# Mixer of a macaron block: rounding the queries and keys of six head pairs as whole tiles, and placing them by transfers

## The chip, the cores and the metric

The kernel runs on one core of one Trainium2 chip. The metric is device time in microseconds (us) for one execution. The kernel before was run three times: 890.2 us is the median, 889.88 and 890.86 the ends. The engines are named as in the profile: PE (TensorE, matrix multiplications), PEld (its weight loads), DVE (VectorE), ACT (ScalarE), POOL (GpSimd) and SP (SyncE, which here only issues transfers); "SPq" in a row is SP's queue of transfers.

## The reference, cut to what matters

```python
for layer in range(DEPTH):                       # DEPTH = 1, x is 512 x 1024, float32
    x = x + 0.5 * swiglu(rmsnorm(x, ffn1_norm), ffn1_w_gate, ffn1_w_up, ffn1_w_down)
    x = x + token_mixer(rmsnorm(x, mix_norm), w_in, w_out, ...)
    x = x + 0.5 * swiglu(rmsnorm(x, ffn2_norm), ffn2_w_gate, ffn2_w_up, ffn2_w_down)
return rmsnorm(x, final_norm)

def token_mixer(h, w_in, w_out, ...):            # 4 differential heads, 8 dilated heads
    qa, ka, va, qb, kb, vb = split(h @ w_in)     # head dimension 64
    oa = diff_attention(qa, ka, va, lam, bias)   # two maps per head: p0 - lam * p1, causal
    ob = dilated_attention(qb, kb, vb, bias)     # three dilations, joined into one softmax
    return concat(rmsnorm(oa) * (1 - lam0), ob) @ w_out
```

The scores are `q @ k.T * 64 ** -0.5` plus a bias, in float32. The change concerns only how q and k reach the score products.

## The kernel before, in words

The span has three stages: the first feed-forward block, the mixer (about 325 to 545 us into the span) and the second feed-forward block. Everything is held transposed: 128 partitions are 128 features, 512 columns are the tokens.

**Split products.** PE multiplies in the format fp32r, which is float32 rounded. Where one rounding is not enough, a value is split into a rounded high part (ACT copies it into an fp32r tile, which rounds it) and the rest (DVE subtracts), and a product is made of three products of parts (`mm3`, lines 152 to 154) or, for the scores, of two.

**The mixer.** A list `plan` names twelve steps, `v0 q0 q1 v1 q2 q3 q4 v2 q5 q6 v3 q7`, each of eight chunks of PE work (48 matmuls of 512 columns in a q step, 96 of 256 columns in a v step). A step `q u` projects the queries and keys of head pair `u` into two PSUM tiles, `pq` and `pk`; each holds two heads (or two maps of one differential head), one in partitions 0 to 63 (`lo`) and one in 64 to 127 (`hi`). There are eight pairs, 0 to 7; pairs 0 to 3 are differential heads. The rest of the mixer is fitted between these chunks by a table: `put(t, rank, f)` asks for step `f` at chunk `t`; steps of a rank under 10 are issued before the chunk, those of a rank of 10 or more behind it, in the order of their ranks. PE, DVE and ACT run their instructions in exactly that order. SP's order is chosen by a scheduler, and it too issues its transfers one after the other: a transfer whose wait isn't over holds up those behind it.

**What the scores read.** For pair `u` the scores need six tiles of 128 partitions: `q0` and `q1`, the two queries, each stacked as high part and rest (`q0`: high part in `lo`, rest in `hi`; `q1` the other way round); `k0` and `k1`, the high part of a key in both halves; `l0` and `l1`, the key's rest in both halves. `score(m, i)` (lines 1227 and 1228) makes, for map or head `m` and the block `i` of 128 queries, two matmuls: `k` against `q`, then `l` against `q`; `q` is the stationary operand. With `e` the last chunk of step `q u`, the first scores of pairs 1 to 6 come ahead of chunk `e + 6`; pairs 1 to 3 ask for both `m` at once, pair 6 for `m = 1` a chunk later, pairs 4 and 5 (named `STACKED`) four chunks later.

**How these tiles are filled before.** Behind chunk `e`, `scaled` (lines 1055 and 1057) takes `pq` and `pk` out of PSUM into `tq` and `tk`, two DVE instructions on 128 partitions. Then there are three ways:

- Pairs 0 and 7 (`evac_now`) do all halves by ACT and DVE. The change leaves them alone.
- Pairs 1 to 4: `evac_q` casts four halves of 64 partitions on ACT (lines 1063 to 1066) right behind chunk `e`; `evac_k` copies the other half of `k0` and `k1` by two transfers, makes the two rests of the keys on DVE (line 1078) and copies each by a transfer (line 1073); `evac_rests` makes the two rests of the queries on DVE (line 1085), a chunk later, writing them straight into `q0` and `q1`.
- Pairs 5 and 6 (`SPREAD`): the keys are cast as one tile `kh` of 128 partitions (line 1114), and their rest is made as one tile `kl` (line 1120); eight transfers of 64 partitions (line 1109) put them into `k0, k1, l0, l1`. The queries are done by halves in place (lines 1125 and 1129).

**What else is in the queues there.** ACT's exponentials of the scores (line 1232), its copies of transposed probabilities `ptb` (line 1256) for the products with the values (`po`, line 1267), its casts of weights (line 944) and of outputs `mh` (line 1307); DVE's score steps (line 1229), weight rests (line 948) and `tx` (line 1358); SP's weight loads (line 139) and bias strips (line 878).

Of the kernel before, what the change touches and what calls it, by code (L numbers as in the profile page):

```python
# [14 lines left out]
F32 = mybir.dt.float32  # L15
F32R = mybir.dt.float32r
# [12 lines left out]
NQ = S // P  # L29
# [53 lines left out]
def tile_macaron(ctx: ExitStack, tc, xs, xT, wf, wgu1, wst1, wd1, wdg1, wqk, wv, wo, wgu2, wst2, wd2,  # L83
# [13 lines left out]
    def slot(i, nm, dt=F32):  # L97
        return sl.tile([P, S], dt, tag=f"slot{i}", name=nm)
# [867 lines left out]
    vt = {}  # L966

    STACKED = (4, 5)
    SPREAD = (5, 6)
    SOONER = (2, 3)  # L970
    DIVS = ((1, 1, 1, 1), (1, 1, 1, 1))
    TURN_AT, VALUES_AT, NEXT = (5, 7, 8), (7, 10), 4
# [60 lines left out]
    def qk_chunks(u):  # L1033
# [12 lines left out]
        def tiles():  # L1046
            b0 = 31 + (u % 2) * 6
            qk[u] = [slot(b0 + i, f"{n}{u}", F32R)
                     for i, n in enumerate(("q0", "q1", "k0", "k1", "l0", "l1"))]
            return qk[u]  # L1050

        def scaled():
            tq = st["tq"] = slot(28, f"tq{u}")
            tk = st["tk"] = slot(30, f"tk{u}")
            V.scalar_tensor_tensor(flat(tq[:]), evens(st["pq"][:]), -(HD ** -0.5),
                                   flat(held["bc"][:]), op0=ALU.mult, op1=ALU.mult)
            V.tensor_tensor(flat(tk[:]), evens(st["pk"][:]), flat(held["bc"][:]), op=ALU.mult)
            return tq, tk

        def evac_q():  # L1060
            q0, q1, k0, k1, l0, l1 = tiles()
            tq, tk = scaled()
            A.copy(k0[lo, :], tk[lo, :])
            A.copy(k1[hi, :], tk[hi, :])
            A.copy(q0[lo, :], tq[lo, :])
            A.copy(q1[hi, :], tq[hi, :])

        def evac_k():
            q0, q1, k0, k1, l0, l1 = qk[u]
            tq, tk = st["tq"], st["tk"]  # L1070

            def other_half(t, a, b):
                nc.sync.dma_start(t[b, :].bitcast(F32), t[a, :].bitcast(F32))

            other_half(k0, lo, hi)
            other_half(k1, hi, lo)
            for a, b, kx, lx in ((lo, hi, k0, l0), (hi, lo, k1, l1)):
                V.tensor_tensor(lx[a, :], tk[a, :], kx[a, :].bitcast(F32), op=ALU.subtract)
                other_half(lx, a, b)

        def evac_rests():
            q0, q1, k0, k1, l0, l1 = qk[u]
            tq = st["tq"]
            for a, b, qx in ((lo, hi, q0), (hi, lo, q1)):
                V.tensor_tensor(qx[b, :], tq[a, :], qx[a, :].bitcast(F32), op=ALU.subtract)

        def evac_now():
            q0, q1, k0, k1, l0, l1 = tiles()
            tq, tk = scaled() if u != 7 else (st["tq"], st["tk"])
# [10 lines left out]
        if u == 7:  # L1100
            put(e, 11, scaled)
            put(e + 1, 2.5, evac_now)
        elif u in DIRECT:
            put(e, 11, evac_now)
        elif u in SPREAD:
            def send(t, *places):
                for o, a in zip(places, (lo, hi)):
                    for b in (lo, hi):
                        nc.sync.dma_start(o[b, :].bitcast(F32), t[a, :].bitcast(F32))

            def cast_k():
                q0, q1, k0, k1, l0, l1 = tiles()
                t = st["kh"] = slot(0, f"kh{u}", F32R)
                A.copy(t[:], st["tk"][:])
                send(t, k0, k1)

            def low_k():
                q0, q1, k0, k1, l0, l1 = qk[u]
                t = slot(1, f"kl{u}", F32R)
                V.tensor_tensor(t[:], st["tk"][:], st["kh"][:].bitcast(F32), op=ALU.subtract)  # L1120
                send(t, l0, l1)

            def cast_q(n):
                a = (lo, hi)[n]
                A.copy(qk[u][n][a, :], st["tq"][a, :])

            def low_q(n):
                a, b = ((lo, hi), (hi, lo))[n]
                V.tensor_tensor(qk[u][n][b, :], st["tq"][a, :], qk[u][n][a, :].bitcast(F32),
                                op=ALU.subtract)  # L1130

            put(e, 11, scaled)
            put(e + 1, 6.7, cast_k)
            put(e + 2, 7, low_k)
            for n in range(2):
                put(e + 2 + n, 6.7, cast_q, n)
                put(e + 3 + n, 11, low_q, n)
        else:
            put(e, 11, evac_q)
            put(e + 1, 11, evac_k)  # L1140
            put(e + 2, 7, evac_rests)
        return [lambda k=k: chunk(k) for k in range(KD)]

    mh, ml, whole, mixed = [None] * KD, [None] * KD, {}, [None] * 4
# [58 lines left out]
    def attention(u, s):  # L1203
# [205 lines left out]
        for i in range(NQ):  # L1409
            for m in range(2):  # L1410
                put(s + step * i + (0 if quick or diff else m), 6, score, m, i)
            put(s + step * i + (1 if quick else 3), 5, combine, i)
            if diff:
                put(tv + 2 * i, 2, turn, 0, i)
                put(tv + 2 * i + (3 if (u, i) in ((0, 0), (1, NQ - 1)) else 2), 1, values, 0, i)
            else:
                for m in range(2):
                    put(tv + step * i + (0 if quick else m), 2, turn, m, i)
                    put(tv + step * i + (1 if quick else m + 2), 1, values, m, i)
# [503 lines left out]
```

## Time and profile before

| what | value |
|---|---|
| median of three runs | 890.2 us |
| the profiled execution: its own time | 890.6 us |
| its span, first to last instruction | 887.7 us, so 2.9 us lie around it |
| mean granted TensorE clock | 0.997 |
| busy over the span: PE, DVE, ACT, POOL | 99%, 85%, 62%, 13% |
| mixer, 320 to 545 us: PE, DVE, ACT busy of 225 us | 222.77, 179.42, 146.44 us |
| DMA share in six stretches of 10 to 13 us in which q and k are placed | 0.44 to 0.76 |

A row of the timeline gives the start in us from the span's start, the time taken in us, the engine, the line, the operation, output<-inputs, shapes and the count; a bracket at the end gives the idle time before it and what ended it. PE's matmuls are pipelined: a matmul of 512 columns shows 0.38 us, but the next one starts 0.22 us after it, so that waits of PE are best read from one start to the next.

### The profile page before, as it was taken

Reading aid. Unit: us, or ns where it says so; the run is one execution under the profiler, and the core shown is the slowest. Engines: PE = TensorE matmul, PEld = TensorE weight load, DVE = VectorE, ACT = ScalarE, POOL = GpSimd, SP = SyncE. Lnnn points to the kernel's source line nnn. Section 1 sums busy time; section 2 is a strip of 40 time slices with the busy share of each in tenths; the row PEclk is TensorE's granted clock in tenths of the full one; section 3 lists DMA queues with packets and bytes.
Section 4 is the critical chain, followed back from the end, with each engine's and each line's share of the span. In section 5 each row is a group of like instructions: output and inputs, shape, how many; then the busy total and the mean of one; then the engine's idle time right before and its main releaser. Section 6 shows DMA issues by size and latency. Waiting matters only on the chain.

```text
span 887.7 us, 17743 instructions
## 1 busy us (share of the span) xinstructions
PE 875.6 (99%) x6558; PEld 834.5 (94%) x6558; DVE 755.1 (85%) x1590; ACT 550.7 (62%) x1162; POOL 111.2 (13%) x140
## 2 busy tenths in 40 slices
PE   9999999999999999999999999999999999999996
PEld 8889999999999999998989889889999999999996
DVE  7799998787998995788997859999899678799786
ACT  7456674455765764666766858466667355666474
POOL 0011101012103100001010220011110111211100
PEclk9999999999999999999999999999999999999998
DMA  8456756688857842445365664656783857884842
GB/s 279 125 168 157 177 142 184 148 212 213 201 141 211 222 132 95 119 131 156 106 174 149 183 139 120 176 158 152 185 212 97 201 169 187 216 224 118 215 127 95
DMA packets 65685, 146.85 MB, mean 165 GB/s; under 512 B 7632, under 2 KB 8912, under 8 KB 65600
## 3 DMA queue, kind: packets, MB, share of 16 engines
q1 hardware_dynamic: 47840, 113.02, 39.2%
q0 software_dynamic: 17616, 32.45, 22.7%
q8 instruction: 51, 0.84, 0.4%
q14 instruction: 34, 0.28, 0.1%
q10 hardware_dynamic: 144, 0.26, 0.1%
HBM read 137.28 MB, written 2.14 MB: 157 GB/s over the span
## 4 chain that ended last, share of the span: by engine, by line
PE 82%; DVE 10%; ACT 4%; issue 2%; DMA 1%; SPq 0%; DVEq 0%; ACTq 0%
PE po L1267 2%; PE pdb L154 1%; DVE w L948 1%; PE pdb L153 1%; PE pdb L152 1%; DVE w L445 1%; PE pv L1012 1%; PE pv L1014 1%; PE pv L1013 1%; PE pygb L152 1%; PE pwgb L154 1%; PE pxgb L154 1%; PE pyub L154 1%; PE pyub L153 1%; PE pxub L154 1%
## 5 line engine op out<-in xcount | busy, mean ns | idle before, releaser
L1232 ACT ACTIVATE pr<-pr,small 128x128 f32<-128x128 f32 (+3 forms) x64 | 35.7, 559 | 31.4 <-DVE small L1229 31.1
L441 ACT CAST w<-s2b 128x512 fp32r<-128x512 f32 x52 | 32.4, 623 | 22.0 <-DVE s2b L423 19.9
L441 ACT CAST w<-s2a 128x512 fp32r<-128x512 f32 x48 | 29.8, 623 | 23.3 <-DVE s2a L423 19.7
L445 DVE TENSOR_TENSOR w<-s2b,w 128x512 fp32r<-128x512 f32 x52 | 35.6, 685 | 0.9 <-ACT w L441 0.6
L1012 PE MATMUL pv<-w,xh 128*128 128x256 f32 x128 | 35.7, 279 | 0.0
L1229 DVE CUSTOM_DVE_ANT_0 pr<-sc,strip 128x128 f32<-128x128 f32 (+3 forms) x64 | 29.5, 485 | 7.2 <-PE sc L1228 7.0
L1014 PE MATMUL pv<-w,xh 128*128 128x256 f32 x128 | 35.1, 274 | 0.0
L1013 PE MATMUL pv<-w,xl 128*128 128x256 f32 x128 | 35.1, 274 | 0.0
L445 DVE TENSOR_TENSOR w<-s2a,w 128x512 fp32r<-128x512 f32 x48 | 32.8, 684 | 0.8 <-ACT w L441 0.6
L152 PE MATMUL pq<-xh,w 128*128 128x512 f32 x64 | 25.6, 401 | 0.0
L948 DVE TENSOR_TENSOR w<-raw_qk,w 128x512 fp32r<-128x512 f32 x32 | 21.7, 686 | 4.5 <-ACT w L944 4.5
L1013 PEld LDWEIGHTS pv<-w,xl 128*128 128x128 f32 x128 | 24.5, 191 | 0.1
L1012 PEld LDWEIGHTS pv<-w,xh 128*128 128x128 f32 x128 | 24.5, 191 | 0.1
L1014 PEld LDWEIGHTS pv<-w,xh 128*128 128x128 f32 x128 | 24.5, 191 | 0.0
L152 PE MATMUL pk<-xh,w 128*128 128x512 f32 x64 | 24.3, 380 | 0.0
L154 PE MATMUL pq<-xh,w 128*128 128x512 f32 x64 | 24.3, 379 | 0.0
L153 PE MATMUL pk<-xl,w 128*128 128x512 f32 x64 | 24.3, 379 | 0.0
L154 PE MATMUL pk<-xh,w 128*128 128x512 f32 x64 | 24.3, 379 | 0.0
L153 PE MATMUL pq<-xl,w 128*128 128x512 f32 x64 | 24.3, 379 | 0.0
L1267 PEld LDWEIGHTS po<-v,ptb 128*128 128x128 f32 x160 | 21.5, 191 | 2.6 <-ACT ptb L1256 1.6
L944 ACT CAST w<-raw_qk 128x512 fp32r<-128x512 f32 x32 | 19.3, 615 | 6.2 <-PE pv L1013 2.8
L1267 PE MATMUL po<-v,ptb 128*128 128x128 f32 (+1 forms) x160 | 22.0, 272 | 1.0 <-ACT ptb L1256 1.0
(826 smaller groups left out, 4096.5 us busy)
## 6 DMA issues: line engine op xcount, KB each, us to landing
raw_qk<-wqk_dram SPq DMA_DIRECT2D x16, 512.0 KB, 3.8
raw0bg<-wst_dram SPq DMA_DIRECT2D x9, 512.0 KB, 5.0
raw0bu<-wst_dram SPq DMA_DIRECT2D x9, 512.0 KB, 5.7
raw_gua<-wgu_dram SPq DMA_DIRECT2D x8, 512.0 KB, 3.6
raw0ag<-wst_dram SPq DMA_DIRECT2D x8, 512.0 KB, 5.0
raw0au<-wst_dram SPq DMA_DIRECT2D x8, 512.0 KB, 5.2
raw0ad<-wdg_dram SPq DMA_DIRECT2D x8, 512.0 KB, 5.9
strip<-bias_rows SPq DMA_DIRECT2D x16, 256.0 KB, 4.0
```

Source lines behind the costliest of these rows:

```text
L152: T.matmul(po, wh, mh, start=first, stop=False, skip_group_check=on)
L153: T.matmul(po, wh, ml, start=False, stop=False, skip_group_check=on)
L154: T.matmul(po, wl, mh, start=False, stop=last, skip_group_check=on)
L441: A.copy(made[t][0], source(t))
L445: V.tensor_tensor(l, source(t), h.bitcast(F32), op=ALU.subtract)
L948: V.tensor_tensor(l[:, c:c + 512], raw[:, c:c + 512], h[:, c:c + 512].bitcast(F32), op=ALU.subtract)
L1012: T.matmul(po, xh[k][:, xs], mh_, start=k == 0, stop=False)
L1013: T.matmul(po, xl[k][:, xs], mh_, start=False, stop=False)
L1014: T.matmul(po, xh[k][:, xs], ml_, start=False, stop=k == KD - 1)
L1229: V.tensor_tensor_reduce(out=o, in0=a, in1=b, op0=ALU.add, op1=ALU.min, scale=1.0, scalar=3.0e38, accum_out=st["mx"][:, m, i:i + 1])
L1232: A.activation(pi, pi, AF.Exp, scale=-1.0, bias=st["mx"][:, m, i:i + 1], accum_out=st["ls"][:, m, i:i + 1])
L1267: T.matmul(st["po3"][:, i, d0:d0 + dn], st["ptb", m, i][:, k * P:(k + 1) * P], vk, start=k == 0, stop=k == i)
```

## The change

Pairs 1 to 6 now all go one way. `scaled` stays where it was. At chunk `e + 1` ACT casts the keys as one tile `kh`, at `e + 2` the queries as one tile `qh`; DVE makes the keys' rest `kl` at `e + 2` and the queries' rest `ql` at `e + 3`. Each of the four tiles lies in a slot that is free at that time, and transfers of 64 partitions by 512 columns put them where the scores read them: four for `kh`, two for `qh`, four for `kl`, two for `ql`, all issued by SP. The scores stay where they were. Besides, the product with the values of pair 0's first query block is asked for one chunk earlier.

For pairs 1 to 4 this takes out four casts, four subtractions and four transfers, and puts in two casts, two subtractions (of 128 partitions) and twelve transfers; for pairs 5 and 6 one cast and one subtraction fewer, and four transfers more.

```diff
-    SPREAD = (5, 6)
...
-        def evac_q():
...
-        def evac_k():
...
-        def evac_rests():
...
-        elif u in SPREAD:
+        else:
+            kt, lt, qt, rt = (20, 21, 22, 23) if u < 5 else (0, 1, 2, 3)
+
             def send(t, *places):
-                for o, a in zip(places, (lo, hi)):
-                    for b in (lo, hi):
-                        nc.sync.dma_start(o[b, :].bitcast(F32), t[a, :].bitcast(F32))
+                for a, o in zip((lo, hi), places):
+                    for p, b in o:
+                        nc.sync.dma_start(p[b, :].bitcast(F32), t[a, :].bitcast(F32))
 
             def cast_k():
                 q0, q1, k0, k1, l0, l1 = tiles()
-                t = st["kh"] = slot(0, f"kh{u}", F32R)
+                t = st["kh"] = slot(kt, f"kh{u}", F32R)
                 A.copy(t[:], st["tk"][:])
-                send(t, k0, k1)
+                send(t, ((k0, lo), (k0, hi)), ((k1, lo), (k1, hi)))
 
             def low_k():
                 q0, q1, k0, k1, l0, l1 = qk[u]
-                t = slot(1, f"kl{u}", F32R)
+                t = slot(lt, f"kl{u}", F32R)
                 V.tensor_tensor(t[:], st["tk"][:], st["kh"][:].bitcast(F32), op=ALU.subtract)
-                send(t, l0, l1)
...
+                send(t, ((l0, lo), (l0, hi)), ((l1, lo), (l1, hi)))
+
+            def cast_q():
+                q0, q1 = qk[u][:2]
+                t = st["qh"] = slot(qt, f"qh{u}", F32R)
+                A.copy(t[:], st["tq"][:])
+                send(t, ((q0, lo),), ((q1, hi),))
+
+            def low_q():
+                q0, q1 = qk[u][:2]
+                t = slot(rt, f"ql{u}", F32R)
+                V.tensor_tensor(t[:], st["tq"][:], st["qh"][:].bitcast(F32), op=ALU.subtract)
+                send(t, ((q0, hi),), ((q1, lo),))
 
             put(e, 11, scaled)
             put(e + 1, 6.7, cast_k)
+            put(e + 2, 6.7, cast_q)
             put(e + 2, 7, low_k)
-            for n in range(2):
-                put(e + 2 + n, 6.7, cast_q, n)
-                put(e + 3 + n, 11, low_q, n)
-        else:
-            put(e, 11, evac_q)
-            put(e + 1, 11, evac_k)
-            put(e + 2, 7, evac_rests)
+            put(e + 3, 7, low_q)
...
-                put(tv + 2 * i + (3 if (u, i) in ((0, 0), (1, NQ - 1)) else 2), 1, values, 0, i)
+                put(tv + 2 * i + (3 if (u, i) == (1, NQ - 1) else 2), 1, values, 0, i)
```

The order of the instructions shows what this does to the queues. On SP, at pair 1, the kernel before has this (a row is the line, the transfer, output<-input and the shape; "x2" is two transfers; `raw_qk` and `strip` are weights and bias from DRAM):

```order
L139 DMA raw_qk_4672<-wqk_dram 128x1024
L1073 DMA k_4457<-k_4457 64x512
L1073 DMA k_4458<-k_4458 64x512
L1073 DMA l_4459<-l_4459 64x512
L1073 DMA l_4460<-l_4460 64x512
L878 DMA strip_4882<-bias_rows 128x512
L878 DMA strip_4884<-bias_rows 128x512
L139 DMA raw_qk_4680<-wqk_dram 128x1024
```

The same place in the changed kernel, where lines have other numbers:

```order
L139 DMA raw_qk_4680<-wqk_dram 128x1024
L1083 DMA k_4471<-kh_4475 64x512 x2
L1083 DMA k_4472<-kh_4475 64x512 x2
L1083 DMA q_4469<-qh_4504 64x512
L1083 DMA q_4470<-qh_4504 64x512
L1083 DMA l_4473<-kl_4508 64x512 x2
L1083 DMA l_4474<-kl_4508 64x512 x2
L1083 DMA q_4469<-ql_4546 64x512
L1083 DMA q_4470<-ql_4546 64x512
L139 DMA raw_qk_4688<-wqk_dram 128x1024
L878 DMA strip_4894<-bias_rows 128x512
L878 DMA strip_4896<-bias_rows 128x512
```

Four transfers have become twelve; the eleventh (`q_4469<-ql`) fills the `hi` half of `q0` and the twelfth the `lo` half of `q1`; a weight load now stands ahead of the two strips. At pairs 2 to 6 the twelve stand together in the same way (at pair 3 one transfer of `kl` is ahead of the two of `qh`).

On ACT, at pair 2, the kernel before has the four casts by halves ahead of a copy of transposed probabilities and of an output:

```order
L1063 CAST k_4821<-tk_4826 64x512
L1064 CAST k_4822<-tk_4826 64x512
L1065 CAST q_4819<-tq_4825 64x512
L1066 CAST q_4820<-tq_4825 64x512
L1256 COPY ptb_4841<-pt_4836 128x512
L1307 ACTIVATE mh_4848<-ot_4843,few 128x512
L944 CAST w<-raw_qk_4770 128x512 x2
```

In the changed kernel the two casts of whole tiles come behind them:

```order
L1228 COPY ptb_4839<-pt_4834 128x512
L1279 ACTIVATE mh_4846<-ot_4841,few 128x512
L1088 CAST kh_4855<-tk_4828 128x512
L944 CAST w<-raw_qk_4778 128x512
L1100 CAST qh_4872<-tq_4827 128x512
L944 CAST w<-raw_qk_4778 128x512
```

So the first cast of a key has moved from ahead of the copies `ptb` and `mh` to behind them, and the cast of the queries a weight cast further.

More of the change, by code (lines that the diff above doesn't have):

```diff
@@ L1058, in scaled @@
             return tq, tk
-        def evac_q():
[L1061 to L1066, printed above, removed]
-        def evac_k():
[L1069 to L1079, printed above, removed]
-        def evac_rests():
[L1082 to L1085, printed above, removed]
         def evac_now():
@@ L1120, in low_k @@
                 V.tensor_tensor(t[:], st["tk"][:], st["kh"][:].bitcast(F32), op=ALU.subtract)
-                send(t, l0, l1)
[L1123 to L1130, printed above, removed]
+                send(t, ((l0, lo), (l0, hi)), ((l1, lo), (l1, hi)))
```

## The prediction

> **What bounds the kernel now.** I read the page first, then the busy time of the mixer in windows, then PE's timeline from one start to the next, because shares say nothing of single waits. The page's first part gives busy time and share of the span:
>
> ```profile
> PE 875.6 (99%) x6558; PEld 834.5 (94%) x6558; DVE 755.1 (85%) x1590; ACT 550.7 (62%) x1162; POOL 111.2 (13%) x140
> ```
>
> The windows over the mixer, 320 to 545 us, end with this sum (length, then the busy time of each engine):
>
> ```profile
> sum 225.00, PE 222.77 PEld 204.93 DVE 179.42 ACT 146.44 POOL 17.93; mean PE 24.75 PEld 22.77 DVE 19.94 ACT 16.27 POOL 1.99
> ```
>
> PE shows 2.2 us idle of 225, DVE 45.6, ACT 78.6. The change works on ACT, DVE and SP; on PE it only moves one matmul. So it can gain no more than PE's waits, and it loses whatever wait it puts in PE's way. The largest old waits behind the work that is removed, in PE's timeline:
>
> ```profile
> 369.33 0.27 PE L1013 MATMUL pv<-w,xl 128*128 128x256 f32 x1
> 369.44 0.28 PE L1014 MATMUL pv<-w,xh 128*128 128x256 f32 x1
> 370.19 0.38 PE L1267 MATMUL po<-v,ptb 128*128 128x128 f32 x1 [0.47 <-ACT ptb L1256]
> ...
> 411.96 0.38 PE L153 MATMUL pk<-xl,w 128*128 128x512 f32 x1
> 412.18 0.38 PE L154 MATMUL pk<-xh,w 128*128 128x512 f32 x1
> 413.06 0.38 PE L1267 MATMUL po<-v,ptb 128*128 128x128 f32 x1 [0.51 <-ACT ptb L1256]
> ...
> 480.82 0.27 PE L1014 MATMUL pv<-w,xh 128*128 128x256 f32 x1
> 481.63 0.30 PE L1350 MATMUL pt<-ident,pr 128*128 128x128 f32 x1 [0.53 <-DVE tx L1358]
> ```
>
> The starts show more than the brackets. A matmul of 256 columns is otherwise followed after 0.11 us (369.33 to 369.44) and one of 512 after 0.22 (411.96 to 412.18), so these waits cost 0.75 - 0.11 = 0.64, 0.88 - 0.22 = 0.66 and 0.81 - 0.11 = 0.70 us, 2.0 together. The releasers are ACT's copy `ptb` and DVE's `tx`, and in both queues casts and rests of q and k stand ahead of them.
>
> **What is removed.** A cast of a half, a rest of a half and a cast of a whole tile (count, shortest, median and longest time in ns):
>
> ```profile
> L1063 ACT CAST k<-tk x4: 617/619/621, 362.4 to 422.4; 64x512 fp32r<-64x512 f32 x4
> L1078 DVE TENSOR_TENSOR l<-tk,k x8: 680/688/691, 363.2 to 423.8; 64x512 fp32r<-64x512 f32 x8
> L1114 ACT CAST kh<-tk x2: 601/610/620, 457.8 to 472.2; 128x512 fp32r<-128x512 f32 x2
> ```
>
> Half a tile costs as much as a whole one. Pairs 1 to 4 lose two casts and two rests each, pairs 5 and 6 one of each: ten casts by 0.62 are 6.2 us of ACT, ten rests by 0.69 are 6.9 us of DVE. Neither engine is the bound, so what counts is PE's waits. Besides the 2.0 us there is one place more, at pair 3's first scores, where four casts (2.5 us) and four rests (2.8 us) had just gone by. Here are the starts of the first scores of pairs 1 to 6, with the matmul before pair 3's:
>
> ```profile
> 370.99 0.36 PE L1227 MATMUL sc<-k,q 128*128 128x256 f32 x1
> ...
> 400.12 0.28 PE L1227 MATMUL sc<-k,q 128*128 128x256 f32 x1
> 400.36 0.28 PE L1227 MATMUL sc<-k,q 128*128 128x256 f32 x1
> ...
> 414.90 0.38 PE L154 MATMUL pk<-xh,w 128*128 128x512 f32 x1
> 415.41 0.39 PE L1227 MATMUL sc<-k,q 128*128 128x256 f32 x1
> 416.02 0.39 PE L1227 MATMUL sc<-k,q 128*128 128x256 f32 x1
> ...
> 432.23 0.28 PE L1227 MATMUL sc<-k,q 128*128 128x256 f32 x1
> ...
> 464.70 0.28 PE L1227 MATMUL sc<-k,q 128*128 128x256 f32 x1
> ...
> 479.27 0.37 PE L1227 MATMUL sc<-k,q 128*128 128x256 f32 x1
> ```
>
> At pair 3, 0.51 - 0.22 = 0.29 us are lost ahead of the first score, and 0.61 instead of pair 2's 0.24 lies between the two maps, another 0.37. All of it together, 0.64 + 0.66 + 0.70 + 0.66 = 2.66 us, is what the change can give back; I take all of it.
>
> **What is added: twelve transfers in one queue.** The first score of a pair reads `q0` whole. Its `hi` half is now filled by the eleventh of twelve transfers that SP issues one by one, and the `lo` half of `q1` by the twelfth; before, DVE wrote them in place. What SP needs for one is shown at pairs 5 and 6, where before sends eight (count at the end), and what a weight load needs is beside it:
>
> ```profile
> 458.42 2.40 SPq L1109 DMA_DIRECT2D k<-kh  x4
> ...
> 472.82 2.40 SPq L1109 DMA_DIRECT2D k<-kh  x4
> 475.31 2.46 SPq L1109 DMA_DIRECT2D l<-kl  x4
> ...
> 345.74 0.33 SPq L139 DMA_DIRECT2D raw_qk<-wqk_dram  x1
> ```
>
> Four take 2.40 us, a pitch of 0.60; at pair 6 the second four follow the first at once, so SP is what they wait for. From issue to landing, for the transfers into `l`:
>
> ```profile
> DMA to landing us min/median/max: 2.2/2.3/4.7
> ```
>
> So `q0` is complete 10 x 0.60 + 2.3 = 8.3 us behind the end of the cast `kh`, and `q1` 0.6 later, as long as `qh`, `kl` and `ql` are ready when SP gets to them (3.6, 2.4 to 3.6 and 6.0 us in); they need three instructions of 0.6 to 0.7 us each and some others between, and only at pair 4 do I find one late.
>
> [...]
>
> When does `kh` end? These rows decide it, in the order of the pairs:
>
> ```profile
> 362.71 0.55 DVE L1229 CUSTOM_DVE_ANT_0 pr<-sc,strip 128x384 f32<-128x384 f32 x1
> 364.93 0.61 ACT L1232 ACTIVATE pr<-pr,small 128x384 f32<-128x384 f32 x1
> ...
> 392.32 0.60 PE L1303 MATMUL ot<-ident,ob 128*128 128x128 f32 x4
> 396.17 0.69 ACT L1307 ACTIVATE mh<-ot,few 128x512 fp32r<-128x512 f32 x1
> ...
> 407.38 0.62 ACT L1063 CAST k<-tk 64x512 fp32r<-64x512 f32 x1 [0.45 <-DVE tk L1057]
> ...
> 422.14 0.60 PE L1250 MATMUL pt<-ident,pr 128*128 128x128 f32 x4
> ...
> 457.78 0.62 ACT L1114 CAST kh<-tk 128x512 fp32r<-128x512 f32 x1
> ...
> 472.19 0.60 ACT L1114 CAST kh<-tk 128x512 fp32r<-128x512 f32 x1
> ```
>
> - Pair 1: the cast now stands behind the exponentials, the second of which needs the DVE step that ends at 363.26: 363.26 + 0.61 + 0.61 = 364.5. `q0` at 372.8, wanted at 370.99 less the old 0.64, 370.35: wait 2.45. The second map is wanted 0.24 behind the first and comes 0.60 behind: 0.36 more. 2.8 us.
> - Pair 2: behind `mh`, which needs the transposes that end at 392.92: plus 0.69 and 0.61, 394.2. `q0` at 402.5, wanted at 400.12: 2.4 + 0.36 = 2.75.
> - Pair 3: nothing in between, 408.0. `q0` at 416.3, wanted at 415.41 less 0.66 and 0.29, 414.46: 1.85 + 0.36 = 2.2.
> - Pair 4: behind `ptb`, whose transposes end at 422.74; with two instructions of 0.6, 423.95, so 432.25 against 432.23. Its `qh` stands behind two exponentials and holds SP up a little, an estimate of 0.4. The second head is wanted four chunks later.
> - Pair 5: 458.4, `q0` at 466.7, wanted at 464.70: 2.0. The second head is late enough.
> - Pair 6: 472.8, `q0` at 481.1, wanted at 479.27: 1.8; the second a chunk later, in time.
>
> The times are the clock of before; a wait moves all behind it alike, so each pair is judged by itself. The sum is 2.8 + 2.75 + 2.2 + 0.4 + 2.0 + 1.8 = 12.0 us. Behind the waiting scores on PE stand the next projections, so nothing runs in their place; DVE's score steps and ACT's exponentials wait with them, and their queues empty meanwhile, which is why I take the whole 2.66.
>
> **What I cost at nothing.** Behind the twelve on SP stand weight loads and strips. They go out some 2 us later, but loads are asked for three units ahead (`load(n + 3)`) and cast four chunks on, over 5 us, while PE itself is late by as much; without that cover each costs its lateness, up to 2 us. The moved matmul with the values stands at the transposes of 366.43 now; its copy `ptb` was made late, behind four casts:
>
> ```profile
> 366.43 0.38 PE L1250 MATMUL pt<-ident,pr 128*128 128x128 f32 x2
> 366.65 0.25 ACT L1256 COPY ptb<-pt 128x128 f32<-128x128 f32 x1
> ```
>
> In the new order it follows `kh` (364.5) and one weight cast: ready at about 365.4, a microsecond early. If that cover were gone PE would wait the difference, some 0.5 us.
>
> **The sum.** 12.0 - 2.66 = 9.3 us on the profiled execution: 887.7 + 9.3 = 897.0 of span, with 2.9 around it 899.9. It lies 0.4 over the median of the runs shown, so 890.2 + 9.3 = **899.5 us**.
>
> **The rivals.** *A, the transfers are in time* (faster). If a half tile is issued as fast as the weight load above, 0.33 us, ten pitches are 3.3 us, less than the smallest room, which is pair 1's 370.35 - 364.5 - 2.3 = 3.55; all waits vanish and the 2.66 remains: 887.5 us. The rooms of pairs 1, 2, 3, 5 and 6 are 3.55, 3.6, 4.15, 4.0 and 4.15, together 19.45; with the second maps the waits are 53 pitches less 20.2, so the point from which it decides is a pitch of 0.43. For it: long rows of twelve do not occur before, and 2.66 us do lie there to be had. Against: three rows of four at 0.60. [...] Chance 0.08.
>
> *B, the pitch is only the bare issue.* Taken singly, the issues of before take less than the pitch (shortest, median and longest in ns):
>
> ```profile
> L1109 SPq DMA_DIRECT2D k<-kh x8: 467/573/602, 458.4 to 474.6; - x8
> ```
>
> With 0.47 the waits are 53 x 0.47 - 20.2 = 4.7, so +2.0: 892.2 us. Against it are the same rows of four. Chance 0.09.
>
> *C, the gaps cost the clock.* At the end of the span PE stops, and the granted clock (seventh entry of a row, behind POOL) falls:
>
> ```profile
> 880.00:880.50 0.50, 0.33 (x3) 0.08 (x1) 0.50 (x2) 0.50 (x1) 0.00 (x0) 1.00 1.05 373
> 883.00:883.50 0.50, 0.00 (x0) 0.00 (x0) 0.00 (x0) 0.00 (x0) 0.00 (x0) 0.70 0.91 367
> ```
>
> PE ends at 880.33, and a mean of 0.70 with a low of 0.50 puts the fall at 883.2, 2.9 us later. My longest gap is 2.45. Half a microsecond more, from a landing at 2.8, and pairs 1 and 2 run at half clock for about as long again, an estimate of 1.4 us each: 899.5 + 2 x (0.5 + 1.4) = 903.3 us. [...] Chance 0.12.
>
> **How the numbers follow.** The forecast has 0.68; by itself it reaches from 897, with the median issue and some waits smaller, to 903, with landings half a microsecond longer. A difference under 0.2%, 1.8 us, is about what cannot be told from no change. Faster is A, 0.08; same is the ground between A and B, 0.03; slower the rest, 0.89. The range of 8 in 10 takes in the forecast, C, and half of what lies towards B: 894 to 904 us.
>
> **What would show it.** Right: in PE's timeline gaps of 2 to 2.5 us ahead of the first scores of pairs 1, 2, 3, 5 and 6, put down to a transfer into `q` from `ql`, and twelve issues of about 7.2 us on SP; the waits at `ptb` and `tx` gone. Wrong: issues under 0.45 us, or scores that start on time; or a granted clock below 1 behind a gap; or casts of weights that wait for a transfer.

## The result, and the profile after

The changed kernel takes 918.3 us, the median of four runs (916.3 to 918.7), beside 890.0 us for the kernel before on the same chip (889.8 to 890.9). The ratio is 1.031, with an interval of 1.0298 to 1.0323. The forecast was slower, 899.5 us in a range of 894 to 904: the direction is right, the size is wrong by 18.8 us. The profiled execution took 918.2 us, with a span of 915.5 and a mean granted clock of 0.987 (before 0.997).

From the page of the changed kernel, the busy times and the group of the scores (the last part of a row is the idle time of PE just before the group, and what ended it):

```profile
PE 884.5 (97%) x6558; PEld 842.3 (92%) x6558; DVE 748.6 (82%) x1580; ACT 545.0 (60%) x1152; POOL 111.2 (12%) x140
...
L1199 PE MATMUL sc<-k,q 128*128 128x256 f32 (+2 forms) x64 | 22.9, 363 | 20.9 <-DMA q<-ql 20.9
```

PE's busy time has grown by 8.9 us although it runs the same 6558 matmuls, and 20.9 us of idle time stand before the scores, all ended by transfers from `ql` into `q`. DVE and ACT are less busy, by 6.5 and 5.7 us, and nothing comes of it. The two numbers of PE are two separate losses. The first, the waits, in PE's timeline, at the first scores of pairs 1 to 6:

```profile
374.24 0.55 PE L1199 MATMUL sc<-k,q 128*128 128x256 f32 x1 [3.91 <-DMA q<-ql]
...
410.43 0.36 PE L1199 MATMUL sc<-k,q 128*128 128x256 f32 x1 [4.12 <-DMA q<-ql]
...
430.71 0.36 PE L1199 MATMUL sc<-k,q 128*128 128x256 f32 x1 [4.42 <-DMA q<-ql]
...
451.26 0.36 PE L1199 MATMUL sc<-k,q 128*128 128x256 f32 x1 [2.09 <-DMA q<-ql]
...
489.53 0.58 PE L1199 MATMUL sc<-k,q 128*128 128x256 f32 x1 [4.30 <-DMA q<-ql]
...
508.03 0.36 PE L1199 MATMUL sc<-k,q 128*128 128x256 f32 x1 [2.02 <-DMA q<-ql]
```

The brackets add up to 20.9; taken from start to start, less the usual distance of 0.11 to 0.33 us, they are 4.08, 4.28, 4.58, 2.25, 4.46 and 2.18, together 21.8 where the forecast had 12.0. The old waits at `ptb` and `tx` in the prediction's first rows are gone.

The second loss is the clock. PE's busy time is in the second number of these windows of the changed kernel, the granted clock (PEclk) behind POOL; the windows have a length of 3.41 us, because all changes of the clock in this trace lie on one grid of 3.413 us (the falls, at 373.28, 410.83, 431.31, 451.79, 489.33 and 912.59 us, are 11, 6, 6, 11 and 124 of these lengths apart):

```profile
core 0: us, PE busy (x) PEld busy (x) DVE busy (x) ACT busy (x) POOL busy (x), PEclk, DMA share, GB/s
369.87:373.28 3.41, 0.45 (x5) 0.21 (x2) 0.47 (x1) 0.48 (x1) 0.00 (x0) 1.00 0.88 204
373.28:376.69 3.41, 2.46 (x11) 2.49 (x12) 0.60 (x4) 0.95 (x4) 0.00 (x0) 0.50 0.89 271
376.69:380.11 3.42, 3.42 (x18) 3.42 (x17) 0.00 (x0) 0.47 (x1) 0.00 (x0) 0.50 0.26 87
...
448.37:451.79 3.42, 1.33 (x12) 1.17 (x11) 1.75 (x9) 0.93 (x5) 0.00 (x0) 1.00 0.67 152
451.79:455.20 3.41, 3.41 (x18) 3.41 (x17) 2.58 (x13) 1.12 (x4) 0.00 (x0) 0.50 0.83 275
...
489.33:492.75 3.42, 3.22 (x9) 2.67 (x10) 0.91 (x3) 1.52 (x4) 0.00 (x0) 0.50 0.24 89
506.40:509.82 3.42, 1.79 (x16) 1.82 (x17) 2.76 (x10) 1.82 (x6) 0.00 (x0) 1.00 0.89 255
```

A window in which PE was busy for 0.45 us (13%) or 1.33 us (39%) is followed by one at half clock; the one with 1.79 us (52%), which holds the wait of pair 6, is not. Pairs 2 and 3 have one window more each at half clock, 410.83 to 414.24 and 431.31 to 434.72, both fully busy, behind windows with 0.40 and 0.60 us of work; pair 5's at 489.33 comes behind one with none. In the six windows PE is busy for 19.3 us. There a matmul of 256 columns is followed after 0.21 us instead of 0.11 and one of 512 after 0.43 instead of 0.22, so half of that time, 9.7 us, is the estimate of the loss. The account: 890.0 + 21.8 of waits - 2.7 given back + 9.7 = 918.8, beside 918.3.

Why the waits are nearly twice those forecast is to be seen on SP (start, length, the number of transfers at the end), at pairs 1 and 6:

```profile
364.50 2.44 SPq L1083 DMA_DIRECT2D k<-kh  x4
366.99 2.02 SPq L1083 DMA_DIRECT2D q<-qh  x2
369.11 2.47 SPq L1083 DMA_DIRECT2D l<-kl  x4
371.67 1.18 SPq L1083 DMA_DIRECT2D q<-ql  x2
...
499.30 2.39 SPq L1083 DMA_DIRECT2D k<-kh  x4
501.79 1.19 SPq L1083 DMA_DIRECT2D q<-qh  x2
503.07 2.48 SPq L1083 DMA_DIRECT2D l<-kl  x4
505.65 1.19 SPq L1083 DMA_DIRECT2D q<-ql  x2
```

The pitch of about 0.6 us is as forecast. At pair 6 the eleventh issue starts 6.35 us behind the first (forecast 6.0) and the score 2.4 us behind that. At pair 1 two issues take 2.02 instead of 1.19 us and the eleventh starts at 7.17; pairs 2 to 5 have 7.1 to 8.0, with one long issue or two. The landings are longer as well. From the start of the eleventh issue to the score it takes 2.4 to 2.9 us in four pairs, 3.6 in pair 5 and 4.5 in pair 3, where 2.3 was forecast. For the transfers into `l`, shortest, median and longest (2.2, 2.3 and 4.7 before):

```profile
DMA to landing us min/median/max: 2.2/2.8/4.6
```

So three things had to be told apart: SP's row, what makes it longer than forecast, and the clock.

### The profile page after: what moved, and what is told of

It reads as the page before. It is cut to its first block, busy times and chain, and to the rows that moved or that the text cites. A ratio compares the mean times of both kernels' runs of the same rounds, so it can differ in the third digit from the quotient of the medians.

```text
span 915.5 us, 17804 instructions
## 1 busy us (share of the span) xinstructions
PE 884.5 (97%) x6558; PEld 842.3 (92%) x6558; DVE 748.6 (82%) x1580; ACT 545.0 (60%) x1152; POOL 111.2 (12%) x140
## 4 chain that ended last, share of the span: by engine, by line
PE 81%; DVE 9%; ACT 4%; DMA 2%; issue 2%; SPq 1%; DVEq 0%; ACTq 0%
DMA q<-ql 2%; PE po L1239 2%; PE pdb L154 1%; PE pdb L152 1%; PE pdb L153 1%; DVE w L445 1%; PE pq L152 1%; PE pq L154 1%; PE pq L153 1%; PE pk L152 1%; PE pk L154 1%; PE pk L153 1%; PE pv L1011 1%; PE pv L1013 1%; PE pv L1012 1%
## 5 line engine op out<-in xcount | busy, mean ns | idle before, releaser
L1199 PE MATMUL sc<-k,q 128*128 128x256 f32 (+2 forms) x64 | 22.9, 363 | 20.9 <-DMA q<-ql 20.9
L1011 PE MATMUL pv<-w,xh 128*128 128x256 f32 x128 | 37.2, 291 | 0.0
L1013 PE MATMUL pv<-w,xh 128*128 128x256 f32 x128 | 36.7, 287 | 0.0
L1199 PEld LDWEIGHTS sc<-k,q 128*128 128x128 f32 x64 | 12.8, 199 | 23.6 <-issue 13.4
L1011 PEld LDWEIGHTS pv<-w,xh 128*128 128x128 f32 x128 | 26.0, 203 | 0.1
L1013 PEld LDWEIGHTS pv<-w,xh 128*128 128x128 f32 x128 | 26.0, 203 | 0.0
L948 DVE TENSOR_TENSOR w<-raw_qk,w 128x512 fp32r<-128x512 f32 x32 | 21.8, 685 | 4.5 <-ACT w L944 4.5
```

The lines of the kernel that those rows point to most:

```text
L1011: T.matmul(po, xh[k][:, xs], mh_, start=k == 0, stop=False)
L1013: T.matmul(po, xh[k][:, xs], ml_, start=False, stop=k == KD - 1)
L1199: T.matmul(ps[:, :n], qs[:, qi], mk, start=True, stop=False)
```

## The experiments

**1. Is the clock a third of the loss?** Idle work for PE in the gaps:

```diff
+            if m == i == 0 and 0 < u < 7:
+                for _ in range(8 if u in (4, 6) else 16):
+                    T.matmul(ps[:], qk[u - 1][0][:, :P], full(qk[u - 1][2][:]), start=True, stop=True)
             T.matmul(ps[:, :n], qs[:, qi], mk, start=True, stop=False)
```

> The changed kernel with idle work for TensorE ahead of the first score of pairs 1 to 6: matmuls of 512 columns with the tiles of the pair before, 16 of them (16 x 0.216 = 3.5 us) for pairs 1, 2, 3 and 5 and 8 (1.7 us) for pairs 4 and 6, into the score's own bank, which the score then starts anew; they wait for nothing and are meant to end before the transfers land. Theory 1 (waits and clock): about 10 of the 28 us are not waits but the half clock behind five gaps, 3.05 + 4 x 1.7 us; the first scores start as late as in the changed kernel, but the granted clock stays near 1, so 918.3 - 9.8 = 908.5 us (905 to 911). Theory 2 (waits alone, the rest of the 28 us is some other loss such as contention): the clock's loss is not there to be had, 918 us or more, up to 922.

Measured: 910.1 us (ratio 1.0224, 1.0207 to 1.0241), 8.3 under the changed kernel. PE's timeline at pair 1, and the windows around it:

```profile
370.31 3.70 PE L1201 MATMUL sc<-k,q 128*128 128x512 f32 x16
374.99 0.36 PE L1202 MATMUL sc<-k,q 128*128 128x256 f32 x1 [0.98 <-DMA q<-ql]
...
372.00:377.00 5.00, 4.02 (x26) 3.37 (x25) 0.60 (x4) 0.88 (x4) 0.00 (x0) 1.00 0.92 250
```

The score still starts late, 4.68 us behind the first of the idle matmuls, but the clock stays at 1.00. The six delays, measured in this way, are 4.68, 4.32, 5.05, 1.73, 4.77 and 3.03, together 23.6; 890.0 + 23.6 - 2.7 = 910.9, with no term for the clock. Theory 1 holds: extra work that computes nothing made the kernel faster by 8.3 us.

**2. Issue or bytes?** Twice the transfers, the same bytes:

```diff
-                        nc.sync.dma_start(p[b, :].bitcast(F32), t[a, :].bitcast(F32))
+                        for r in (0, 32):
+                            i, j = (slice(z.start + r, z.start + r + 32) for z in (b, a))
+                            nc.sync.dma_start(p[i, :].bitcast(F32), t[j, :].bitcast(F32))
```

> The changed kernel with each of the twelve transfers of a pair cut in two by rows (32 x 512 in place of 64 x 512): twice the transfers, the same rows and bytes. Theory 1 (SP's issue sets the pitch of 0.60 to 0.65 us, so much for every transfer): the train grows by 11 x 0.62 = 6.8 us ahead of the transfer waited for, in each of six pairs, so about 918.3 + 6 x 6.8 = 959 us (950 to 970). Theory 2 (the DMA engines drain bytes at about 215 GB/s, and SP is held back by them): each issue takes half as long, the train stays as it is, 918 us within 4.

Measured: 960.6 us (1.0776 to 1.0808). SP's row and the DMA queue of 373.4 to 380.8 (packets, MB, share of the sixteen engines' time), and the first score of pair 1:

```profile
373.35 4.96 SPq L1085 DMA_DIRECT2D l<-kl  x8
...
q1 hardware_dynamic: 563, 0.76, 41.0%
...
381.15 0.55 PE L1201 MATMUL sc<-k,q 128*128 128x256 f32 x1 [10.60 <-DMA q<-ql]
```

Eight issues of 64 KB take 4.96 us, 0.62 each, as long as with 128 KB, while the DMA engines are busy for 41%. SP is the limit here, and its price is per transfer.

**3. Is it the place in the row?** The six that the first score needs go first:

```diff
-                send(t, ((q0, hi),), ((q1, lo),))
+                send(t, ((q0, hi),), ())
+                send(st["kh"], (), ((k1, lo), (k1, hi)))
+                send(st["qh"], (), ((q1, hi),))
+                send(st["kl"], (), ((l1, lo), (l1, hi)))
+                send(t, (), ((q1, lo),))
```

(and the earlier three calls of `send` with the first map's places alone).

> The same twelve transfers, in another order: the six that the first score needs (two of k0, two of l0, two of q0) first, then the six of the second map. Theory 1 (the wait is for a place in the row of transfers, nothing else): the first score waits for the sixth transfer, some 2.2 to 3.3 us sooner, where the rest of q now comes last; in pairs 4, 5 and 6, whose second head comes later, 2.2 + 2.5 + 2.2 = 6.9 us go, and the half clock behind two or three of these gaps, 1.7 us each; in pairs 1 to 3 the second map follows at once, so the wait only moves behind the first map. 918.3 - 6.9 - 3.4 to 5.1 = 907 us (903 to 910). Theory 2 (it is the load that twelve transfers put on the memory and the engines, wherever they stand in the row): 916 us or more.

Measured: 909.7 us (1.0205 to 1.0236). PE's timeline at pair 1:

```profile
371.28 0.35 PE L1203 MATMUL sc<-k,q 128*128 128x256 f32 x1 [0.60 <-DMA q<-ql]
375.07 0.55 PE L1203 MATMUL sc<-k,q 128*128 128x256 f32 x1 [3.30 <-DMA q<-ql]
```

The first map now starts 3 us sooner and the second one takes over the wait, as expected. In pair 4, whose second head comes later, nothing is left of it, in pairs 5 and 6 1.8 and 1.0 us. Theory 1 holds, at the upper end of its range.

**4. The keys alone.** The queries are rounded in place by halves, as pairs 5 and 6 did before:

```diff
-            put(e + 2, 6.7, cast_q)
             put(e + 2, 7, low_k)
-            put(e + 3, 7, low_q)
+            for n in range(2):
+                put(e + 2 + n, 6.7, cast_q, n)
+                put(e + 3 + n, 11, low_q, n)
```

> Of the change only the keys: in pairs 1 to 6 kh and kl are rounded whole and sent by eight transfers, while ACT and DVE round the queries in place by halves, as pairs 5 and 6 did before. Theory 1 (the length of the row sets the waits): the last transfer that a first score needs is the sixth (kh + 5 x 0.63 + 2.6 = 5.8 us, wanted 5.9 to 6.5 behind kh), in time but for some tenths; the second map of pairs 1 to 3 needs the eighth, 7.0 us, about 1 us late each; 3 to 3.5 us of waits, no fall of the clock, and some 1.3 of the 2.66 given back: 890 + 2 = 892 us (889.5 to 894.5). Theory 2 (each transfer costs its share of the 28 us, in order or not): four pairs of the six get new transfers, two more each than before and slower ones, about 900 to 909 us.

Measured: 894.2 us (1.0031 to 1.0061). What is left of the waits, in PE's timeline, at the two maps of pairs 1 and 2:

```profile
371.40 0.35 PE L1198 MATMUL sc<-l,q 128*128 128x256 f32 x1 [0.93 <-DMA l<-kl]
372.64 0.36 PE L1198 MATMUL sc<-l,q 128*128 128x256 f32 x1 [0.66 <-DMA l<-kl]
...
404.19 0.36 PE L1198 MATMUL sc<-l,q 128*128 128x256 f32 x1 [0.86 <-DMA l<-kl]
405.87 0.36 PE L1198 MATMUL sc<-l,q 128*128 128x256 f32 x1 [1.20 <-DMA l<-kl]
```

Four of twelve transfers fewer, and 24 of 28 us are gone: theory 1, the row's length against the room. The time is 2.2 over the expectation, near its upper end; one window behind pair 1 ran at half clock (mean granted clock of the profiled run 0.996, in run 1 0.999), which I had not counted.

**5. A second queue.** The transfers from `qh` and `ql` on GpSimd's queue:

```diff
-                send(t, ((q0, hi),), ((q1, lo),))
+                send(t, ((q0, hi),), ((q1, lo),), queue=nc.gpsimd)
```

(`qh` likewise).

> The changed kernel, but the four transfers of qh and ql are issued by GpSimd's queue, the eight of kh and kl by SP; the same twelve transfers, rows and bytes. Theory 1 (SP's issue is the limit): the second queue runs beside the first. The last of SP's eight lands kh + 7 x 0.63 + 2.6 = 7.0 us, q0 is whole some 3.3 us behind ql, and against the rooms of 5.9 to 6.5 us there remain about 1 to 1.7 us in pairs 1, 2, 3, 5 and 6, together some 7; the 2.66 come back; the clock falls behind none or one: 890 + 4.5 = 894.5 us (891 to 900). Theory 2 (the DMA engines, 0.9 busy at 205 to 220 GB/s, are the next limit right behind SP): 1.5 MB still need 7 us, and it stays over 910 us.

Measured: 913.7 us (1.0239 to 1.0284). My expectation failed, and theory 2's number came. The DMA queues of 366 to 371 us (q1 is SP's, q0 GpSimd's), and the landings into `l` and `q`:

```profile
q1 hardware_dynamic: 459, 0.74, 54.3%
q0 software_dynamic: 180, 0.51, 36.3%
...
DMA to landing us min/median/max: 2.3/4.1/5.9
...
DMA to landing us min/median/max: 2.5/3.8/7.0
```

With two queues the DMA engines are busy for 91% of this stretch, and over the whole run a transfer into `l` or `q` lands after some 4 us in the median instead of 2.4 to 2.8. SP finishes sooner, but the weight loads and strips behind its row go out sooner too (the load of 372.95 us before 371, landing after 4.9) and share the engines. Of the 28 us the second queue gave back 4.6.

**6. GpSimd's own transfers.** The sums `mx` of pairs 0 to 3 written by ACT, without transfers:

```diff
-            nc.gpsimd.dma_start(w[:], mh[u][:].bitcast(F32))
-            nc.gpsimd.dma_start(w[:], ml[u][:].bitcast(F32), accum_op=ALU.add)
+            A.activation(w[:], st["ot"][:], AF.Copy, scale=sub8[:])
```

> The changed kernel without GpSimd's own transfers (the sums mx of mh and ml of pairs 0 to 3, 2 x 256 KB each), which run beside the trains of pairs 2, 3 and 5; ACT writes mx from the transposes instead, scaled (mh and ml added give the same but for rounding), four activations of 0.7 us. Theory 1 (these transfers crowd the trains): landings of 2.7 to 4.0 us in pairs 2, 3 and 5 fall to 2.3, the long issues of pair 5 too, together 3 to 4 us, and perhaps one window at half clock of 1.7 less: 912 to 915 us. Theory 2 (the lateness comes from SP's own stalls, one issue of 1.1 to 1.9 us in each pair but the last): 917 to 919 us.

Measured: 909.2 us (1.0193 to 1.0245). At pairs 3 and 5 the waits fall by half:

```profile
426.87 0.36 PE L1199 MATMUL sc<-k,q 128*128 128x256 f32 x1 [2.21 <-DMA q<-ql]
...
481.92 0.39 PE L1199 MATMUL sc<-k,q 128*128 128x256 f32 x1 [2.20 <-DMA q<-ql]
```

The six brackets are 4.21, 2.91, 2.21, 2.01, 2.20 and 2.01, together 15.6 instead of 20.9: 5.3 us were crowding by these transfers. They are gone from pairs 2, 3 and 5, whose waits in a repeat of the changed kernel (run 8) differ by 0.3 us at most. Theory 1, but the time fell by 9.1 us where I had expected 3 to 6: only three windows ran at half clock instead of six, by the estimate of 1.7 us for each some 5 us, and I had allowed for one.

**7. The keys alone, on two queues.** Run 4 with the transfers from `kl` on GpSimd's queue:

```diff
-                send(t, ((l0, lo), (l0, hi)), ((l1, lo), (l1, hi)))
+                send(t, ((l0, lo), (l0, hi)), ((l1, lo), (l1, hi)), queue=nc.gpsimd)
```

> The version with the keys alone (894.2 us, which waits for l about 4.5 us in pairs 1 and 2 and loses one window at half clock, 1.7 us), with the four transfers of kl of each pair on GpSimd's queue instead of SP's. Theory 1 (a place in SP's row is what is short): l is whole some 5 us behind kh, in time in every pair; 894.2 - 6.2 = 888.0 us (887 to 890), faster than both kernels by some 2 us. Theory 2 (GpSimd issues slower or its transfers land later than SP's): the waits stay or grow, 893 us or more.

Measured: 897.6 us (1.0063 to 1.0093), slower than run 4. Theory 2's number, for the reason of run 5: GpSimd issues four in 2.12 us, no slower than SP, but they land after 3.6 us in the median instead of run 4's 2.5.

```profile
365.93 2.12 POOL L1083 DMA_DIRECT2D l<-kl  x4 [66.08 <-PE sc L1198]
...
DMA to landing us min/median/max: 2.1/3.6/6.2
```

**8. Whose clock is it?** The changed kernel once more, without an edit.

> The changed kernel once more, to see the clock. In its trace all falls and rises of the granted clock lie on one grid of 3.413 us, and the clock halves for the window after one in which PE was busy for 39% or less, while 52% and more kept it. Theory 1 (the grid runs on its own, not tied to the program or to the start of a gap): the waits before the first scores are as before within 0.5 us, the grid stands elsewhere, and of pairs 4 and 6 (2.25 and 2.18 us) one or the other may come out differently; the falls come at other distances behind the start of the gaps, by up to 3.4 us. Theory 2 (a gap counts from its own start, and 2.2 us is the limit): the falls come as far behind the start of each gap as before.

Measured: one run of 920.1 us. Its windows, on its own grid of 3.413 us, at pairs 4 and 6:

```profile
450.73:454.14 3.41, 1.69 (x15) 1.53 (x15) 2.07 (x13) 0.96 (x4) 0.00 (x0) 1.00 0.81 239
454.14:457.56 3.42, 3.42 (x33) 3.42 (x32) 3.21 (x14) 1.19 (x4) 0.00 (x0) 1.00 0.52 150
505.35:508.76 3.41, 1.53 (x14) 1.29 (x13) 2.98 (x11) 2.77 (x8) 0.00 (x0) 1.00 0.89 204
508.76:512.18 3.42, 3.29 (x29) 3.32 (x30) 2.69 (x10) 1.89 (x7) 0.00 (x0) 1.00 0.70 241
```

The grid stands elsewhere (at pair 1 the fall came 2.9 us behind the start of the gap in the first profile and 5.1 in this one), and pair 4's wait, 1.72 us by its bracket, now keeps the clock: its window is half busy. Pair 6's window of 45% keeps it too. The waits are as before within 0.5 us but for pair 1, 4.98 instead of 3.91. Run 6 has both outcomes in one trace; the windows of its pairs 4 and 5, on its grid:

```profile
443.66:447.07 3.41, 1.40 (x13) 1.31 (x12) 2.03 (x12) 0.68 (x3) 0.00 (x0) 1.00 0.88 229
447.07:450.49 3.42, 3.42 (x18) 3.42 (x18) 3.21 (x14) 1.19 (x5) 0.00 (x0) 0.50 0.69 195
477.79:481.21 3.42, 1.93 (x9) 1.34 (x8) 1.51 (x3) 1.27 (x3) 0.00 (x0) 1.00 0.90 207
481.21:484.62 3.41, 2.70 (x14) 2.46 (x15) 1.54 (x6) 1.70 (x5) 0.00 (x0) 1.00 0.63 205
```

The gap of 2.01 at pair 4 (the first two rows) lies in one window, leaves 41% of it busy and costs the clock; the longer one of 2.20 at pair 5 lies across two windows, leaves 56 and 79%, and does not. Theory 1 holds; a limit on a gap's length (theory 2) does not.

**9 and 10. Half the bytes, on one queue and on two.** Only 32 of 64 rows are sent, the rest of the tiles is zero:

```diff
-                        nc.sync.dma_start(p[b, :].bitcast(F32), t[a, :].bitcast(F32))
+                        i, j = (slice(z.start, z.start + 32) for z in (b, a))
+                        nc.sync.dma_start(p[i, :].bitcast(F32), t[j, :].bitcast(F32))
...
+            def blank():
+                for t in tiles():
+                    G.memset(t[:].bitcast(F32), 0.0)
+
+            put(e - 4, 0, blank)
```

> The changed kernel with twelve transfers of half the bytes: each brings 32 of the 64 rows (64 KB in place of 128 KB); the other rows of the tiles are set to zero by GpSimd four chunks sooner, so half of what the scores add up is left out. Theory 1 (SP's issue of 0.59 us stays, and what made the trains longer than forecast, long issues and late landings, is DMA engines that 128 KB every 0.6 us keep full): the eleventh issue comes 6.0 us behind kh, landings are 2.0 us, so the first scores wait about 2.4, 2.35, 1.8, 0 to 0.8, 1.95 and 1.8 us, some 10.7 instead of 21.8, with one or two windows at half clock: 900 us (897 to 904). Theory 2 (the engines have room; SP stalls for another reason): the waits stay, 914 us or more.

> The same twelve transfers of half the bytes, with those of qh and ql on GpSimd's queue. Theory 1 (two limits lie at the same place, SP's issue at 0.6 us and the DMA engines at 128 KB in 0.6 us, so that a second queue alone, 913.7 us, and fewer bytes alone do not do it): with both taken away the row is kh + 7 x 0.6 + 2.0 = 6.2 us against rooms of 5.9 to 6.5, waits of some tenths and about 1 us for the second maps of pairs 1 to 3: 891 us (889 to 895). Theory 2 (GpSimd's queue is itself slow or late): 905 us or more.

Measured: 907.6 us (1.0177 to 1.0210) and 895.7 us (1.0043 to 1.0074). The first lies between the two theories: the median landing is 2.0 to 2.1 us as expected, but long issues remain (the six brackets are 3.65, 2.81, 2.94, 1.26, 2.35 and 1.74, together 14.8), and four windows ran at half clock where I had allowed for one or two. So full DMA engines are not what causes all of them. The second is 0.7 over theory 1's range; in its trace a wait of 0.6 us is put down to the zeros that GpSimd writes only for this edit. The four together, all with twelve transfers a pair (taken on different chips, on which the kernel before had 890.0 to 891.1 us):

| | one queue | two queues |
|---|---|---|
| 128 KB each | 918.3 | 913.7 |
| 64 KB each | 907.6 | 895.7 |

The second queue is worth 4.6 us with full transfers and 11.9 with half of them. Two limits lie close together: SP's issue of 0.6 us, and DMA engines that need nearly as long for 128 KB (an estimate from run 5's rows: 1.25 MB in 5 us at 91% busy, so about 0.5 us).

**11. The way of before in two more pairs.** Keys sent and queries in place for pairs 3 and 4 too, pairs 1 and 2 left as they were:

```diff
-    SPREAD = (5, 6)
+    SPREAD = (3, 4, 5, 6)
```

(with places 20 and 21 for `kh` and `kl` of pairs 3 and 4).

> The kernel before, with the way of pairs 5 and 6 (keys rounded whole and sent by eight transfers, queries in place by halves) for pairs 3 and 4 as well, where the version with the keys alone showed hardly a wait (0.5 us at pair 3), and not for pairs 1 and 2, where it waited 4.5 us and lost a window at half clock. Theory 1 (what bounds is the room ahead of each first score): the waits of 0.66 and 0.66 us around pair 3's casts go, 0.5 is left: 889.2 us, 0.8 under the kernel before (888.5 to 889.8). Theory 2 (transfers of keys cost time in any pair): slower than before, 891 us or more.

Measured: 889.4 us (11 runs; ratio 0.9991, 0.9983 to 1.0000). Two of PE's waits between 320 and 560 us (total, times, longest):

```profile
PE po L1267 <- ACT ptb L1256: 0.5, 1, 0.5
PE sc L1228 <- DMA l<-kl: 0.4, 1, 0.4
```

One of the two waits at `ptb` (1.0 together before) is gone and 0.4 at a transfer has come. The sign agrees with theory 1, but the difference is under the 0.2% that can be told from none.

**12. The moved values.** The one edit that the prediction cost at nothing, undone:

```diff
-                put(tv + 2 * i + (3 if (u, i) == (1, NQ - 1) else 2), 1, values, 0, i)
+                put(tv + 2 * i + (3 if (u, i) in ((0, 0), (1, NQ - 1)) else 2), 1, values, 0, i)
```

> The changed kernel with the values of pair 0's first row block back where they stood, one chunk later. The prediction cost this move at nothing. If so: 918.3 us within 1.5; if the earlier place makes PE wait for the copy ptb, 0.5 us less, which this run can hardly tell; over 2 us either way would be against the prediction's step.

Measured: 916.8 us (915.9 to 917.0), within the spread of the changed kernel (916.3 to 918.7). No cost can be seen.

**13. Do the parts add up?** Runs 1 and 6 in one, with 8 idle matmuls for all pairs but the first:

> The changed kernel with both edits that took something back: without GpSimd's transfers (909.2 us by itself) and with idle work for TensorE ahead of the first scores (910.1 by itself; 16 matmuls of 0.216 us for pair 1, 8 for the others). Theory 1 (the 28 us are three sums that add up: the row's waits, the crowding by GpSimd's transfers of 5.3 us, and the windows at half clock): without the crowding the waits are 15.5 us as in the run without GpSimd's transfers, and no window falls, so 890 + 15.5 - 2.7 = 903 us (901.5 to 905); against the forecast of 899.5 what is left is SP's own long issues in pairs 1 to 4. Theory 2 (there is a further cost that these two edits only shift about): 907 us or more.

Measured: 905.6 us (1.0158 to 1.0192), 0.6 over theory 1's range. The delays, from the first idle matmul to the score, are 4.99, 3.10, 2.82, 1.80, 3.13 and 3.48, together 19.3, and 889.7 + 19.3 - 2.7 = 906.3: waits alone make the time, to within 0.7 us. They are longer than the 15.6 of run 6 where SP has a long issue. Two pieces of SP's row, each with the only packet of a queue of instructions that moved in that stretch (pair 6, 490.8 to 494.7; pair 2, 402.7 to 406.0):

```profile
490.86 3.67 SPq L1083 DMA_DIRECT2D l<-kl  x4
...
q8 instruction: 1, 0.02, 2.4%
...
402.76 2.67 SPq L1083 DMA_DIRECT2D l<-kl  x4
...
q14 instruction: 1, 0.01, 1.2%
```

Four issues take 3.67 us in the one and 2.67 in the other. In this trace each of the four pairs with an issue longer by 0.7 us or more (1, 4, 5 and 6) has a packet of q8 there, and pairs 2 and 3 have neither. Run 6 agrees: its three long issues (at 367.61, 420.25 and 441.44 us) start within 0.12 us of a packet of q8, and no other packet of q8 falls into one of its rows of twelve. In the changed kernel three of six long issues have one (pairs 1, 3 and 4); the other three, in pairs 2, 3 and 5, are those that went with GpSimd's transfers in run 6. Whether SP waits for these packets was not tried by itself.

## Why the prediction was wrong

- **Place and releaser: right.** All six first scores wait for `ql` into `q0`, and only there; the freed time of ACT and DVE bought nothing but PE's old waits.
- **The 2.66 us given back: right.** The old waits are gone from the trace, and the accounts of runs 1 and 13 close to within 0.9 us with that term.
- **The pitch of 0.60 us and its cause: right.** Run 2 shows SP's price per transfer, so rivals A and B, which lived from a shorter pitch, fall.
- **"10 x 0.60 pitch + 2.3 landing" for each pair: too small.** I took the row of pair 6 of the kernel before, where nothing else moves, for all pairs. 21.8 us of waits stand against 12.0. Of the 9.8 between, 5.3 are the transfers of GpSimd that run beside the trains of pairs 2, 3 and 5 (run 6). The other 4.5 are, as far as the rows show, long issues on SP (in run 6 still in pairs 1, 3 and 4, together 3.1 us over 0.6 each), a row that is a little longer even where no issue is long (run 6, pairs 5 and 6: the eleventh starts 6.37 and 6.35 us behind the first instead of 6.0, some 2 us in six pairs), and 0 to 0.3 us more than 2.3 from the eleventh issue to the score. Against them stand the 0.36 us that I added for the second map of pairs 1 to 3: no wait is shown there. Why SP has the long issues stays open (run 13). Pair 4, which I cost at 0.4, waits 2.25. At pair 6, which has neither GpSimd's transfers nor a long issue, 1.8 was forecast and 2.18 came.
- **"My longest gap is 2.45", with the fall 2.9 us behind PE's last work: wrong, and the failing step that weighs as much.** I read these 2.9 us as a length that a gap must have, which was my estimate from the one fall at the end of the span, and so put the clock at nothing in the sum. In the traces the clock changes on a grid of 3.413 us that stands elsewhere in runs 6 and 8, and the falls follow how much of one window is idle: run 6 has 41% busy and a fall behind a gap of 2.01, 56 and 79% busy and none behind one of 2.20. Nor was the window idle throughout: 39% busy came ahead of the fall at 451.79 above. Five of the six gaps, 2.25 to 4.58 us long, cost six windows at half clock, 9.7 us by the estimate; filling them gave back 8.3 us. Rival C had the half clock behind a gap, but as a matter of the gap's length, for two pairs and 1.4 us each.
- **What I cost at nothing: right.** Run 12 shows no cost of the moved values, and in the changed kernel no cast of a weight holds up PE behind SP's row.

With the measured terms the sum is 890.0 + 12.0 + 5.3 + 4.5 - 2.7 + 9.7 = 918.8; the 4.5 in it is what is left of the waits, not a measurement of its own.

## What to carry to other kernels

A step that is cheap for the engines may be dear in transfers: count the transfers that one queue must issue between the producer and the first reader, take the pitch from a row in the trace, and then ask which other queue's transfers run in the same microseconds in each place, rather than take one undisturbed row for all. When a stall of PE is forecast, look at the granted clock behind it too: here five of six gaps cost six windows at half clock, by the estimate 9.7 us on top of 21.8 of waits, 1.7 for a fully busy window. And order or thin out a row of transfers (runs 3 and 4) before giving it a second queue, which gave back 4.6 us in run 5, where the DMA engines were busy for 91%, and nothing in run 7.

## What the runs showed of the hardware

- The clock's windows: in the traces of the changed kernel and of runs 6, 7 and 8, between 355 and 545 us, each of the 14 windows at full clock in which PE was busy for 41% or less was followed by half clock, and none with 43% or more was; the lowest of these had 43% (run 6, 423.18 us) and 45% (run 8, 505.35). Run 4 does not fit: it lost a window behind pair 1, where two waits of 0.93 and 0.66 us take only 1.59 of the 3.41 us of a window that holds them both. At half clock a window of 72% did not bring the full clock back (373.28 above), one of 94% did (489.33).
- A transfer of 64 rows of 2 KB between places on the chip costs SP 0.59 to 0.62 us, and so does one of 32 rows; it lands after 2.3 us in the median where GpSimd's transfers are left out (run 6; 2.0 with 32 rows, run 2), and after some 4 us, up to 7, in run 5, where the DMA engines were 0.9 busy.
